# Reordering the products of a pair in the seven-product loops: B22 second, T4 after B21, the pair ends T2, T1, T3

## The chip, the core and the metric

The kernel runs on one core of a Trainium2 chip. A core has a matrix engine (TensorE, PE in the profile; its weight loads are listed apart as PEld), VectorE (DVE), ScalarE (ACT), GpSimd (POOL) and SyncE (SP, here a queue that issues transfers). Each engine works through its own list of instructions in order and waits where an operand is not ready. The metric is the device time of one execution in microseconds (us), the median of several runs; before the change it is 1209.62 us (three runs, 1209.15 to 1214.17).

## The reference

One layer of a decoder trunk is computed for 512 prompt tokens and 32 sample tokens (544 together, `NT`), width 1024, feed-forward width 2816, all in float32. The parts that the change touches are the big weight products: the input projection (keys, values, queries, convolution inputs, merge gates) and the feed-forward part.

```python
h = rmsnorm(x, w['norm1']) * (1 + sc1) + sh1
bg, cg, xin, q, kc, vc, ks, vs, kw, vw, nsa_g, merge_g = split_columns(h @ w['w_in'])
...
x = x + g1 * ((ga * y_a + gb * y_b) @ w['w_out'])
h2 = rmsnorm(x, w['norm2']) * (1 + sc2) + sh2
x = x + g2 * ((jax.nn.silu(h2 @ w['w_gate']) * (h2 @ w['w_up'])) @ w['w_down'])
```

## The kernel before

**Seven products in place of eight.** A weight slab of 256 output columns is cut into four blocks (two halves of the output columns, two halves of the contraction), the activations into four blocks (two halves of the contraction, two halves of the 544 tokens, `WH` = 272 each). Two by two blocks would take eight block products; Winograd's scheme takes seven and some sums. One slab handled so is called a pair here (it gives two times 128 output columns). The function `wpair` (L339) works one off. Its products, in three PSUM tiles: into `wA` go B11 (weights W0), then, added on top, T2 (weights WY), T3 (WZ) and T4 (W3); into `wB` goes B21 (W0); into `wC` go T1 (WY) and, on top, B22 (WZ). The names are those of the moving operands: B11, B21, B22 are blocks of the activations, T1 to T4 are sums of blocks, prepared once. W0 is two raw blocks of the slab, WY and WZ are sums of blocks that VectorE forms for each pair (tile `ws`), W3 is one raw block.

**Three matmuls for one.** To keep float32 accuracy each weight and each activation is split into a high and a low part (`to_hilo`, L393: ScalarE copies the high part, VectorE subtracts it for the low part) and `mm3` (L251) issues high x high, high x low, low x high: L252, L253, L254 in the profile. A block product is 12 matmuls of 128x272 (4 contraction chunks x 3), or 9 in the eight pairs of the down projection. A pair is 84 matmuls (63 in the down projection). In the profile `wh`/`wl` and `Wh`/`Wl` are the high and low weight tiles from two pools with two buffers each; W0 and WZ take `wh`/`wl`, WY and W3 take `Wh`/`Wl`.

**Snapshots.** `wA` is read in the middle of its accumulation: `snap` (L298) copies it with ScalarE to one of four buffers (L301 in the profile) after B11 (s1), after T2 (s2) and after T3 (s3). The next product into `wA` has to wait until the copy is done. The function `out(m, q, p, s)` finishes a quarter of the result: out(0,0) adds `wB` and s1, out(1,1) adds `wC` (holding T1 alone) and s3, out(0,1) adds `wC` (now with B22) and s2, out(1,0) takes `wA` after T4. B22 may be added to `wC` only after out(1,1) has read it. What `out` does further depends on the loop: `pair_out` (L887), `gate_out` (L1721), `up_out` (L1734), `up_seven` (L1752), `dn_out` (L1819).

**Pairs overlap.** `wpair` is a generator. Its first step issues B11 and B21, its second T2, T1 and T3; T4 and B22 are left in the generator `rest`, kept in `late[0]`, and are issued within the next pair. The callers advance `late[0]` once between the two steps (L951, L1847, L1856, L1864), which issued T4 of the last pair; `wpair` itself advances it behind T1 (L372), which issued B22 of the last pair. So the written order was B11, B21, T4 (last pair), T2, T1, B22 (last pair), T3.

**Two loops use it.** The first (L936, 23 pairs) computes the input projection in about 129 to 390 us; the second (L1840, 28 pairs) the feed-forward part in about 850 to 1156 us, with a plain product (`down_plain`) of some 45 us in it. Between them lies the attention. In the second loop six pairs of `up` form the sums of blocks of the feed-forward activations as well (`up_seven`: buffers `t0`, `t1`, `t3`, tiles `fs`, `f_x`), since the down projection is done by seven products, too.

**What sets the order.** The program is written as above, and a scheduling layer then orders the instructions of each engine by its own estimate of when operands are ready; it may bring single matmuls of a later product forward. Once built, each engine's order is fixed, and waits are semaphores. Transfers of weight slabs (`raw`, three buffers) and of prepared sums (`ws<-pre`) are issued by SP in order.

Of the kernel before, what the change touches and what calls it, by code (L numbers as in the profile page):

```python
# [14 lines left out]
ALU = mybir.AluOpType  # L15
# [23 lines left out]
WH = 272  # L39
# [117 lines left out]
def build(tc, a, o):  # L157
    nc = tc.nc
    sync, act, dve, pool, pe = nc.sync, nc.scalar, nc.vector, nc.gpsimd, nc.tensor
# [14 lines left out]
    def lin_ps(nm):  # L174
        return ps.tile([128, 512], F32, tag="g", bufs=5, name=nm)
# [12 lines left out]
    def nm(s):  # L188
        uid[0] += 1
        return f"{s}_{uid[0]}"  # L190
# [87 lines left out]
    Q = (slice(0, WH), slice(WH, NT))  # L278
# [5 lines left out]
    def seven(o_, ww, wlp, wsp):  # L284
        wi, ns, late = [0], [0], [iter(())]
        hooks = iter(o_.splits)

        def wsplit(view, odd=None):
            nk = view.shape[1]
            if odd is None:  # L290
                wi[0] += 1
                odd = wi[0] % 2
            pools = ((wpool, "wh"), (wpool, "wl")) if odd else ((ww, "Wh"), (wlp, "Wl"))
            wh, wl = (p_.tile([128, 8, 128], F32R, tag=t, bufs=2, name=nm(t))[:, 0:nk, :] for p_, t in pools)
            to_hilo(view, wh, wl)
            return wh, wl

        def snap(p):  # L298
            t = o_.snaps[ns[0] % 4]
            ns[0] += 1  # L300
            o_.snap_ops.append(act.activation(t, p, AF.Copy))  # L301
            return t

        def product(p, w, k0, X, first):
            n_ = len(X[0]) if isinstance(X[0], list) else 4
            xk = lambda t, k: t[k] if isinstance(t, list) else t[:, k, :]
            k0 *= n_
            for k in range(n_):
                mm3(p, w[0][:, k0:k0 + n_], w[1][:, k0:k0 + n_], xk(X[0], k), xk(X[1], k), k, first and k == 0, k == n_ - 1, skip_group_check=not first)

        def wslab(*key):
            n_ = len(SLABS[key][1]) // 4
            if key in pre:
                t = wsp.tile([128, 16, 128], F32, tag="ws", bufs=2, name=nm("ws"))
                sync.dma_start(t[:, n_:3 * n_].rearrange("p k f -> p (k f)"), pre[key][:, 0:256 * n_])
                y, z = t[:, 0:2 * n_], t[:, 2 * n_:4 * n_]
            else:
                y, z = (wsp.tile([128, 8, 128], F32, tag="ws", bufs=3, name=nm("ws"))[:, 0:2 * n_] for _ in range(2))
            raw = slab(*key)
            q = raw.rearrange("p k f -> p (k f)").rearrange("p (n k f) -> p n k f", n=4, k=n_)  # L320
            return q, y, z, key in pre

        def prepare(slabs):

            raw, y, z, summed = slabs
            n_ = raw.shape[2]
            y1, y2, z1, z2 = y[:, 0:n_], y[:, n_:2 * n_], z[:, 0:n_], z[:, n_:2 * n_]
            a22, a21, a11, a12 = (raw[:, i] for i in range(4))
            W0 = wsplit(raw[:, 2:4].rearrange("p n k f -> p (n k) f"))
            if not summed:  # L330
                dve.tensor_add(y2, a21, a22)
            dve.tensor_add(y1, y2, a11)
            WY = wsplit(y)
            if not summed:
                dve.tensor_add(z1, a11, a21)
            dve.tensor_add(z2, y1, a12)
            return W0, WY

        def wpair(slabs, out, ready=None, o_=o_, tie=None):  # L339

            raw, y, z, summed = slabs
            n_ = raw.shape[2]
            y1, y2, z1, z2 = y[:, 0:n_], y[:, n_:2 * n_], z[:, 0:n_], z[:, n_:2 * n_]
            a22, a21, a11, a12 = (raw[:, i] for i in range(4))
            W0 = wsplit(raw[:, 2:4].rearrange("p n k f -> p (n k) f")) if ready is None else ready[0]
            pA = s_ps(nm("wA"))[:, 0:WH]
            product(pA, W0, 0, o_.B11, True)
            s1 = snap(pA)
            pB = lin_ps(nm("wB"))[:, 0:WH]
            product(pB, W0, 1, o_.B21, True)  # L350
            out(0, 0, pB, s1)
            yield
            if ready is None:
                if not summed:
                    dve.tensor_add(y2, a21, a22)
                with tc.issue_after(tie.ins) if tie else ExitStack():
                    dve.tensor_add(y1, y2, a11)
                WY = wsplit(y)
                if not summed:
                    dve.tensor_add(z1, a11, a21)  # L360
                with tc.issue_after(tie.ins) if tie else ExitStack():
                    dve.tensor_add(z2, y1, a12)
            else:
                WY = ready[1]
            WZ = wsplit(z)
            W3 = wsplit(a22)
            product(pA, WY, 0, o_.T2, False)
            s2 = snap(pA)
            next(hooks, lambda: None)()
            pC = lin_ps(nm("wC"))[:, 0:WH]  # L370
            product(pC, WY, 1, o_.T1, True)
            next(late[0], None)  # L372
            next(hooks, lambda: None)()
            product(pA, WZ, 0, o_.T3, False)
            s3 = snap(pA)
            out(1, 1, pC, s3)
            next(hooks, lambda: None)()

            def rest():
                product(pA, W3, 0, o_.T4, False)  # L380
                out(1, 0, pA, None)
                yield
                product(pC, WZ, 1, o_.B22, False)
                out(0, 1, pC, s2)
                yield
            late[0] = rest()
            yield
        return SimpleNamespace(wsplit=wsplit, wslab=wslab, wpair=wpair, late=late, prepare=prepare)

    def hcols(hf):  # L390
        return slice(*HS[hf])

    def to_hilo(src, hi, lo):  # L393
        act.activation(hi, src, AF.Copy)  # L394
        return dve.tensor_sub(lo, src, hi.bitcast(F32))  # L395
# [304 lines left out]
    fins, late = [], []  # L700
# [29 lines left out]
    for n, (b, v) in enumerate(STEPS):  # L730
# [17 lines left out]
        if n:  # L748
            ready_ = late[:1] if n == 1 else late
            late = late[len(ready_):]  # L750
# [1001 lines left out]
    def up_seven(G, c2):  # L1752
        if c2 % 3 == 2:
            tt = [f_x[:, 4 * i:4 * i + 4] for i in range(2)]
            bb = [f_x[:, 8 + i] for i in range(6)]
        else:
            late_ = c2 % 3 == 0
            tt = [f6_tile(3 * late_ + i, [128, 4, WH], F32R, "fs") for i in range(2)]
            bb = [t[:, i] for t in (f6_tile(3 * late_ + 2, [128, 4, WH], F32R, "fs"), f6.tile([128, 2, WH], F32R, tag=f"fg{late_:d}", bufs=1, name=nm("fs"))) for i in range(t.shape[1])]
        ops = fops.setdefault((c2 - 2) // 3, {n: ([], []) for n in ("B11", "B21", "B22", "T1", "T2", "T3", "T4")})  # L1760
        for n, i in (("B11", 0), ("B21", 2), ("B22", 4)):
            for x in range(2):
                ops[n][x].append(bb[i + x])
        for n, t, i in (("T1", 0, 0), ("T3", 0, 1), ("T2", 1, 0), ("T4", 1, 1)):
            for x in range(2):
                ops[n][x].append(tt[t][:, 2 * x + i])
        Uf = flat(U)

        def out(m, q, p, s_):
            if s_ is None:  # L1770
                dve.scalar_tensor_tensor(G[:, 1, Q[0]], p, -1.0, G[:, 1, Q[0]], ALU.mult, ALU.mult)
                to_hilo(G[:, 1, Q[0]], bb[2], bb[3])
                return
            dve.tensor_add(U[:, m, Q[q]], p, s_)
            if m == 1:
                dve.scalar_tensor_tensor(G[:, 1, Q[1]], U[:, 1, Q[1]], -1.0, G[:, 1, Q[1]], ALU.mult, ALU.mult)
                to_hilo(G[:, 1, Q[1]], bb[4], bb[5])
            elif q == 1:
                dve.tensor_mul(G[:, 0, :], U[:, 0, :], G[:, 0, :])
                t0, t1, t3 = Uf[:, 0:WH], Uf[:, 2 * WH:3 * WH], Uf[:, 3 * WH:4 * WH]  # L1780
                dve.tensor_sub(t0, G[:, 0, Q[0]], G[:, 0, Q[1]])
                dve.tensor_sub(Uf[:, WH:2 * WH], G[:, 1, Q[1]], G[:, 0, Q[1]])
                to_hilo(G[:, 0, Q[0]], bb[0], bb[1])
                pair = lambda i: Uf[:, 2 * i * WH:2 * i * WH + 2 * WH].rearrange("p (k n) -> p k n", k=2)
                dve.scalar_tensor_tensor(t1, t0, -1.0, G[:, 1, Q[1]], ALU.mult, ALU.subtract)
                dve.scalar_tensor_tensor(t3, G[:, 1, Q[0]], -1.0, t1, ALU.mult, ALU.subtract)
                to_hilo(pair(0), tt[0][:, 0:2], tt[0][:, 2:4])
                to_hilo(pair(1), tt[1][:, 0:2], tt[1][:, 2:4])
        return out

    def gated(t, c, src, m, g):
# [238 lines left out]
```

## Time and profile before

| | |
|---|---|
| median of three runs | 1209.62 us |
| the profiled execution | 1209.88 us |
| its span (first to last instruction) | 1208.1 us |
| first seven-product loop | about 129 to 390 us |
| attention, output projection, first feed-forward columns | about 390 to 850 us |
| second seven-product loop | about 850 to 1156 us |
| last part of the down projection, final norm, stores | about 1156 to 1208 us |

The profile is one execution; all rows below are from it. A row of the timeline gives start, duration, engine, line, operation, output and inputs, and in brackets how long the engine was idle before it and what ended that. A row of the table by windows gives for one stretch of time its length and, for PE, PEld, DVE, ACT and POOL, the busy time and the number of instructions, then the granted clock, the share of the transfer engines and GB/s.

### The profile page before, as it was taken

What the parts mean: (1) busy time and instruction counts of PE and PEld (TensorE: products, weight loads), DVE (VectorE), ACT (ScalarE), POOL (GpSimd) and SP (SyncE); (2) the same over time, 40 slices, a digit from 0 to 9 for tenths busy, and PEclk for the clock granted to TensorE, in tenths of its full rate; (3) what the DMA queues carried; (4) which work ended last, traced back from release to release, by engine and by line L of the source; (5) the groups of instructions that cost most, each with busy time, mean ns of one, the idle gap of its engine ahead of it and who ended that gap; (6) DMA issues with size and microseconds to landing.
All of it is one profiled execution on the core that took longest, in us unless ns stands there. A gap on an engine that the chain in (4) does not pass through costs nothing. (4 is left out here: it accounts for less than half of the span.)

```text
span 1208.1 us, 25725 instructions
## 1 busy us (share of the span) xinstructions
PE 1191.2 (99%) x10114; PEld 1096.6 (91%) x10114; DVE 849.8 (70%) x1927; ACT 647.6 (54%) x1302; POOL 101.7 (8%) x154
## 2 busy tenths in 40 slices
PE   9999999999999999999999999999999999999997
PEld 7999999999999888787777879999999999999996
DVE  2539976888775576686767866758746877876776
ACT  1416544565456333386766765528555666666542
POOL 1000240000000111120101100000020001001000
PEclk9999999999999999999999999999999999999999
DMA  9953655889655998979887878534475359439512
GB/s 325 370 223 124 203 167 161 261 237 251 201 176 191 365 327 299 312 203 264 234 222 216 220 209 285 201 126 167 110 182 197 136 181 262 149 129 252 197 53 75
DMA packets 82251, 255.63 MB, mean 212 GB/s; under 512 B 9032, under 2 KB 17096, under 8 KB 67930
## 3 DMA queue, kind: packets, MB, share of 16 engines
q1 hardware_dynamic: 69442, 229.85, 54.5%
q0 software_dynamic: 12112, 23.09, 11.7%
q8 instruction: 79, 1.29, 0.4%
q10 hardware_dynamic: 576, 1.05, 0.3%
q14 instruction: 42, 0.34, 0.1%
HBM read 223.15 MB, written 65.28 MB: 239 GB/s over the span
## 5 line engine op out<-in xcount | busy, mean ns | idle before, releaser
L301 ACT ACTIVATE work<-wA 128x272 f32<-128x272 f32 x153 | 60.0, 392 | 85.3 <-PE wA L254 81.5
L395 DVE TENSOR_TENSOR Wl<-ws,Wh 128x1024 fp32r<-128x1024 f32 (+1 forms) x51 | 60.7, 1190 | 47.3 <-ACT Wh L394 44.0
L1417 ACT ACTIVATE P<-P,nms 128x384 f32<-128x384 f32 (+3 forms) x120 | 65.0, 543 | 19.8 <-DVE nms L1416 19.1
L1416 DVE CUSTOM_DVE_ANT_0 P<-sp,ta 128x384 f32<-128x384 f32 (+3 forms) x120 | 52.1, 468 | 30.0 <-PE sp L1404 22.8
L252 PE MATMUL lin<-h_h,wh 128*128 128x288 f32 (+1 forms) x240 | 71.5, 298 | 0.0
L395 DVE TENSOR_TENSOR wl<-ws,wh 128x1024 fp32r<-128x1024 f32 (+1 forms) x51 | 60.3, 1182 | 15.8 <-ACT wh L394 14.6
L253 PE MATMUL lin<-h_l,wh 128*128 128x288 f32 (+1 forms) x240 | 69.2, 289 | 0.0
L254 PE MATMUL lin<-h_h,wl 128*128 128x288 f32 (+1 forms) x240 | 68.9, 288 | 0.0
L394 ACT ACTIVATE wh<-raw 128x1024 fp32r<-128x1024 f32 (+2 forms) x55 | 55.4, 1007 | 24.1 <-PE wC L253 16.9
L394 ACT ACTIVATE Wh<-ws 128x1024 fp32r<-128x1024 f32 (+1 forms) x51 | 52.3, 1025 | 29.9 <-PE wC L253 29.2
L394 ACT ACTIVATE wh<-ws 128x1024 fp32r<-128x1024 f32 (+1 forms) x51 | 52.4, 1027 | 29.1 <-PE wB L253 27.4
L247 ACT ACTIVATE wh<-raw 128x1024 fp32r<-128x1024 f32 (+1 forms) x43 | 41.9, 973 | 43.3 <-PE lin L253 24.4
L395 DVE TENSOR_TENSOR wl<-raw,wh 128x1024 fp32r<-128x1024 f32 (+2 forms) x55 | 63.4, 1153 | 1.8 <-ACT wh L394 1.7
L658 PE MATMUL phi<-gt,wphi 128*128 128x128 f32 x512 | 61.4, 277 | 0.5 <-DMA gt<-in_cache_cmp 0.5
L658 PEld LDWEIGHTS phi<-gt,wphi 128*128 128x128 f32 x512 | 59.1, 192 | 2.7 <-DMA gt<-in_cache_cmp 1.3
L248 DVE TENSOR_TENSOR wl<-raw,wh 128x1024 fp32r<-128x1024 f32 (+1 forms) x43 | 48.2, 1121 | 16.9 <-ACT wh L247 16.4
L252 PE MATMUL wA<-S_hi,Wh 128*128 128x272 f32 x184 | 55.3, 301 | 1.7 <-ACT work L301 1.6
L557 POOL DMA_DIRECT2D pre<-in_wt x28 | 27.3, 977 | 331.0 <-DMA pre<-in_wt 331.0
L254 PE MATMUL wA<-S_hi,Wl 128*128 128x272 f32 x184 | 53.2, 289 | 0.0
L253 PE MATMUL wA<-S_lo,Wh 128*128 128x272 f32 x184 | 53.0, 288 | 0.0
L252 PEld LDWEIGHTS lin<-h_h,wh 128*128 128x128 f32 x240 | 45.6, 190 | 7.5 <-issue 6.2
L253 PEld LDWEIGHTS lin<-h_l,wh 128*128 128x128 f32 x240 | 45.2, 188 | 0.1
(583 smaller groups left out, 4365.6 us busy)
## 6 DMA issues: line engine op xcount, KB each, us to landing
raw<-in_wt SPq DMA_DIRECT2D x88, 1024.0 KB, 6.6
sraw<-in_cache_sel SPq DMA_DIRECT2D x64, 256.0 KB, 4.8
gt<-in_cache_cmp SPq DMA_DIRECT2D x60, 256.0 KB, 5.8
pre<-in_wt SPq DMA_DIRECT2D x20, 512.0 KB, 7.3
pre<-in_wt POOLq DMA_DIRECT2D x20, 512.0 KB, 7.1
ws<-pre SPq DMA_DIRECT2D x20, 512.0 KB, 3.4
raw<-in_wt SPq DMA_DIRECT2D x12, 768.0 KB, 5.7
wraw<-in_cache_winT SPq DMA_DIRECT2D x8, 1024.0 KB, 7.2
```

Of the source, the lines that this page charges most:

```text
L247: act.activation(oh, view, AF.Copy)
L248: dve.tensor_sub(ol, view, oh.bitcast(F32))
L252: pe.matmul(p, lhsT=wh[:, k, :], rhs=xh, start=start, stop=False, **kw)
L253: pe.matmul(p, lhsT=wh[:, k, :], rhs=xl, start=False, stop=False, **kw)
L254: pe.matmul(p, lhsT=wl[:, k, :], rhs=xh, start=False, stop=stop, **kw)
L301: o_.snap_ops.append(act.activation(t, p, AF.Copy))
L394: act.activation(hi, src, AF.Copy)
L395: return dve.tensor_sub(lo, src, hi.bitcast(F32))
L557: pool.dma_start(dst, src, accum_op=ALU.add)
L658: pe.matmul(po[:, c0:c0 + 128], lhsT=w[:, ch], rhs=x[:, :, ch * 16:ch * 16 + 16], start=(n_ == 0 and ch == 0), stop=(n_ == 2 and ch == 7))
L1416: p_ops.append(dve.tensor_tensor_reduce(out=t[:, 0:n], in0=sps[br], in1=t_dist[:, 512 - n:512], scale=-hs, scalar=3e38, op0=ALU.add, op1=A ...
L1417: e_ops.append(act.activation(t[:, 0:n], t[:, 0:n], AF.Exp, scale=-1.0, bias=nms[:, c:c + 1], accum_out=sums[:, c:c + 1]))
```

## The change

In the first step of `wpair`, behind B11 and its snapshot, `late[0]` is advanced once; behind T1 it is run to its end. `rest` now issues B22 first and T4 second. With the callers' advance between the steps the written order becomes B11, B22 (last pair), B21, T4 (last pair), T2, T1, T3. In `up_seven` the sums that need the result of T4 (`t3`, and the split of the second pair of sums) move from out(0,1), which came last, to out(1,0), which comes last now. No instruction is added or removed.

```diff
@@ wpair
             product(pA, W0, 0, o_.B11, True)
             s1 = snap(pA)
+            next(late[0], None)
             pB = lin_ps(nm("wB"))[:, 0:WH]
             product(pB, W0, 1, o_.B21, True)
             out(0, 0, pB, s1)
...
             product(pC, WY, 1, o_.T1, True)
-            next(late[0], None)
+            for _ in late[0]:
+                pass
             next(hooks, lambda: None)()
             product(pA, WZ, 0, o_.T3, False)
             s3 = snap(pA)
...
             def rest():
+                product(pC, WZ, 1, o_.B22, False)
+                out(0, 1, pC, s2)
+                yield
                 product(pA, W3, 0, o_.T4, False)
                 out(1, 0, pA, None)
-                yield
-                product(pC, WZ, 1, o_.B22, False)
-                out(0, 1, pC, s2)
                 yield
@@ up_seven
+        t0, t1, t3 = Uf[:, 0:WH], Uf[:, 2 * WH:3 * WH], Uf[:, 3 * WH:4 * WH]
+        pair = lambda i: Uf[:, 2 * i * WH:2 * i * WH + 2 * WH].rearrange("p (k n) -> p k n", k=2)
 
         def out(m, q, p, s_):
             if s_ is None:
                 dve.scalar_tensor_tensor(G[:, 1, Q[0]], p, -1.0, G[:, 1, Q[0]], ALU.mult, ALU.mult)
                 to_hilo(G[:, 1, Q[0]], bb[2], bb[3])
+                dve.scalar_tensor_tensor(t3, G[:, 1, Q[0]], -1.0, t1, ALU.mult, ALU.subtract)
+                to_hilo(pair(1), tt[1][:, 0:2], tt[1][:, 2:4])
                 return
...
                 dve.scalar_tensor_tensor(t1, t0, -1.0, G[:, 1, Q[1]], ALU.mult, ALU.subtract)
-                dve.scalar_tensor_tensor(t3, G[:, 1, Q[0]], -1.0, t1, ALU.mult, ALU.subtract)
                 to_hilo(pair(0), tt[0][:, 0:2], tt[0][:, 2:4])
-                to_hilo(pair(1), tt[1][:, 0:2], tt[1][:, 2:4])
```

The scheduling layer makes the following of it. The first piece is TensorE before the change, in the second loop, where `wA_1723` is the gate pair of the loop's fourth round (`c2` = 4) and `wA_1740`, `wB_1741` belong to the up pair behind it: the end of T3, then the start of the up pair.

```order
L254 MATMUL wA_1723_11850<-T3_hi_10523,wl_1728_11900 128x272
L252 MATMUL wA_1740_11984<-h2_hi_9891,wh_1738_11980 128x272
L253 MATMUL wA_1740_11984<-h2_lo_9892,wh_1738_11980 128x272
L252 MATMUL wB_1741_11998<-h2_hi_9891,wh_1738_11980 128x272
L253 MATMUL wB_1741_11998<-h2_lo_9892,wh_1738_11980 128x272
L252 MATMUL wA_1723_11850<-h2_hi_9891,Wh_1729_11903 128x272
L253 MATMUL wA_1723_11850<-h2_lo_9892,Wh_1729_11903 128x272
L254 MATMUL wA_1723_11850<-h2_hi_9891,Wl_1730_11904 128x272
L254 MATMUL wA_1740_11984<-h2_hi_9891,wl_1739_11981 128x272
```

Behind T3 stood only four matmuls of the next pair's B11 and B21 (those that need the high weights alone), and then the first three of T4 of the old pair, which go into the tile `wA_1723` whose snapshot s3 had only just been started.

The second piece is the same place after the change: the end of the up pair's B11 (its twelve matmuls stand together directly behind T3) and what follows.

```order
L252 MATMUL wA_1740_11984<-h2_hi_9891,wh_1738_11980 128x272
L253 MATMUL wA_1740_11984<-h2_lo_9892,wh_1738_11980 128x272
L254 MATMUL wA_1740_11984<-h2_hi_9891,wl_1739_11981 128x272
L252 MATMUL wC_1731_11944<-h2_hi_9891,wh_1727_11923 128x272
L253 MATMUL wC_1731_11944<-h2_lo_9892,wh_1727_11923 128x272
L254 MATMUL wC_1731_11944<-h2_hi_9891,wl_1728_11924 128x272
L252 MATMUL wC_1731_11944<-h2_hi_9891,wh_1727_11923 128x272
```

Now B22 of the gate pair (into `wC_1731`) follows B11, then the twelve of B21, and T4 stands 36 matmuls behind T3. No low-weight matmul is left out of B11 and put off.

The third piece is VectorE before the change, around the first reading of `wC_1731` by out(1,1) (L1727); `Wl` and `wl` are low-weight splits of the coming pairs.

```order
L395 TENSOR_TENSOR Wl_1743_12027<-ws_1732_11972,Wh_1742_12026 128x1024
L1774 TENSOR_TENSOR work_10832<-wC_1718_11797,work_10832 128x272
L395 TENSOR_TENSOR wl_1739_11981<-raw_1733_11974,wh_1738_11980 128x1024
L1779 TENSOR_TENSOR work_10832<-work_10832 128x544
L1727 TENSOR_TENSOR work_10832<-wC_1731_11920,work_10832 128x272
```

And after the change, the same reading, L1729 there (the file is two lines longer from here on):

```order
L1777 SCALAR_TENSOR_TENSOR work_10832<-work_10832 128x272
L397 TENSOR_TENSOR wl_1739_11981<-raw_1733_11974,wh_1738_11980 128x1024
L397 TENSOR_TENSOR fs_1705_11722<-work_10832,fs_1705_11722 128x544
L1729 TENSOR_TENSOR work_10832<-wC_1731_11944,work_10832 128x272
L397 TENSOR_TENSOR Wl_1743_12041<-ws_1732_11972,Wh_1742_12040 128x1024
```

The split `wl_1739` (W0 of the up pair) stands further ahead of the reading, with the split of the down projection's sums (`fs`) between them; the split `Wl_1743` (WY of the up pair) has gone from ahead of it to behind it. In 21 of the first loop's 23 pairs and 18 of the second loop's 28 a split of WY (`Wl<-ws`, of the coming pair) still stands directly ahead of this reading after the change.

More of the change, by code (lines that the diff above doesn't have):

```diff
@@ L1779, in out @@
                 dve.tensor_mul(G[:, 0, :], U[:, 0, :], G[:, 0, :])
-                t0, t1, t3 = Uf[:, 0:WH], Uf[:, 2 * WH:3 * WH], Uf[:, 3 * WH:4 * WH]
                 dve.tensor_sub(t0, G[:, 0, Q[0]], G[:, 0, Q[1]])
@@ L1783, in out @@
                 to_hilo(G[:, 0, Q[0]], bb[0], bb[1])
-                pair = lambda i: Uf[:, 2 * i * WH:2 * i * WH + 2 * WH].rearrange("p (k n) -> p k n", k=2)
                 dve.scalar_tensor_tensor(t1, t0, -1.0, G[:, 1, Q[1]], ALU.mult, ALU.subtract)
-                dve.scalar_tensor_tensor(t3, G[:, 1, Q[0]], -1.0, t1, ALU.mult, ALU.subtract)
                 to_hilo(pair(0), tt[0][:, 0:2], tt[0][:, 2:4])
-                to_hilo(pair(1), tt[1][:, 0:2], tt[1][:, 2:4])
         return out
```

## The prediction

> **What bounds the kernel now.** The first view is the page's busy table.
>
> ```profile
> span 1208.1 us, 25725 instructions
> ...
> PE 1191.2 (99%) x10114; PEld 1096.6 (91%) x10114; DVE 849.8 (70%) x1927; ACT 647.6 (54%) x1302; POOL 101.7 (8%) x154
> ```
>
> TensorE is the bound by far: the time can only fall where TensorE waits, and by as much as it waits there. By PE busy there is hardly anything to gain (1208.1 - 1191.2 = 16.9 us in all, the start and the end included), and the list of PE's waits, the second view, is as short:
>
> ```profile
> PE wA L252 <- ACT work L301: 2.5, 4, 1.0
> PE wA L254 <- DVE wl L395: 0.9, 2, 0.5
> PE wA L254 <- DVE Wl L395: 0.5, 2, 0.3
> ```
>
> That is 3.9 us. But a matmul's row lasts 0.29 us while the next starts 0.125 us later, so that a wait of up to 0.16 us leaves no hole in it. The third view, the table by windows, therefore matters more: it has the weight loads (second busy column), one ahead of each matmul and with less overlap.
>
> ```profile
> 153.00:390.00 237.00, 236.59 (x1878) 232.66 (x1877) 175.97 (x261) 129.05 (x195) 20.67 (x26) 1.00 0.69 204
> 930.00:1156.00 226.00, 226.00 (x1755) 221.28 (x1754) 174.47 (x299) 143.75 (x249) 13.75 (x16) 1.00 0.58 181
> 133.00:153.00 20.00, 17.89 (x135) 17.02 (x136) 19.77 (x28) 8.33 (x13) 6.93 (x7) 1.00 0.78 225
> 850.00:930.00 80.00, 78.38 (x608) 76.43 (x607) 47.46 (x77) 42.14 (x75) 6.91 (x8) 1.00 0.57 167
> 942.90:948.80 5.90, 5.90 (x49) 5.90 (x49) 4.29 (x7) 3.49 (x6) 0.00 (x0) 1.00 0.59 186
> ```
>
> The last row is a stretch inside one pair: no hole in either column. In the two steady stretches of the loops (first two rows) the loads are idle 237.00 - 232.66 = 4.34 us and 226.00 - 221.28 = 4.72 us, where PE busy shows 0.41 and 0. The timeline of one change of pairs, the fourth view, shows where.
>
> ```profile
> 948.74 0.29 PE L254 MATMUL wA<-T_hi,wl 128*128 128x272 f32 x1
> 948.87 0.29 PE L252 MATMUL wA<-h_hi,wh 128*128 128x272 f32 x1
> 949.00 0.29 PE L253 MATMUL wA<-h_lo,wh 128*128 128x272 f32 x1
> 949.07 0.40 ACT L301 ACTIVATE work<-wA 128x272 f32<-128x272 f32 x1 [0.57 <-PE wA L254]
> 949.12 0.29 PE L252 MATMUL wB<-h_hi,wh 128*128 128x272 f32 x1
> 949.25 0.28 PE L253 MATMUL wB<-h_lo,wh 128*128 128x272 f32 x1
> 949.52 0.19 PEld L252 LDWEIGHTS wA<-h_hi,Wh 128*128 128x128 f32 x1 [0.21 <-ACT work L301]
> 949.52 0.39 PE L252 MATMUL wA<-h_hi,Wh 128*128 128x272 f32 x1
> 949.75 0.29 PE L253 MATMUL wA<-h_lo,Wh 128*128 128x272 f32 x1
> 949.88 0.29 PE L254 MATMUL wA<-h_hi,Wl 128*128 128x272 f32 x1
> ```
>
> T3 ends with the first row. Its snapshot s3 can start only at 949.07 and ends at 949.47; T4's first matmul, four places behind T3, waits for it until 949.52. It starts 0.27 us after the one ahead instead of 0.125, and the next comes 0.23 us later instead of 0.125: 0.145 + 0.105 = **0.25 us lost per change of pairs**, of which the load's row shows 0.21.
>
> A rule of the Trainium skill bears on each of these two points. Its page "Perfetto Trace Analysis", section "Identifying the Most-Contended Engine", says that matmul busy time is no measure of TensorE's headroom and that the busy share of LDWEIGHTS should be used. By matmul busy the change could win 3.9 us at most, by the loads some 10; the rows above bear the rule out. Its page "TensorE: Matmul & The Clock Gate", section "Step-by-step: what each phase is for", says that TensorE pulls a weight load ahead of running matmuls when it goes to the background buffer. By that rule the second of the two losses would not be there, the first term of the sum below would be 10.8 x 0.145/0.25 = 6.3 us and the time 1206.8; here the load at 949.52 waited along with its matmul and the next start took 0.23 us, so the measurement decides against it.
>
> **The change, part by part.** Nothing is added or removed; each part is a wait that goes or comes.
>
> *T4 behind B21* (both loops). T4 moves from 4 to 6 matmuls behind T3 to 36, or 4.5 us, and the snapshot needs 949.52 - 948.87 = 0.65 us from T3's end. This wait goes in every pair. So do the waits for W0's low part (`PE wA L254 <- DVE wl`) that come with it: B22 of the pair before, whose weights held the buffer of the coming W0, comes 48 matmuls or 6 us earlier. Scaled by 0.25/0.21 the idle times are 4.34 x 1.19 = 5.2 and 4.72 x 1.19 = 5.6: **-10.8 us** in the steady stretches.
>
> *B22 in second place* brings a new wait. B22 is added to `wC`, which out(1,1) must have read, and that reading needs s3. Let T be the start of the first matmul behind T3. B22 is due at T + 12 x 0.125 = T + 1.51. s3 ends at T + 0.60 (949.47 against 948.87), and a reading right behind it would take 0.43 us and be over at T + 1.06. But in 39 of 51 pairs a split of WY stands directly ahead of the reading on VectorE, and it waits for T1. What that costs, the timeline has:
>
> ```profile
> 945.74 0.29 PE L254 MATMUL wC<-T_hi,Wl 128*128 128x272 f32 x1
> 945.94 1.06 ACT L394 ACTIVATE Wh<-ws 128x1024 fp32r<-128x1024 f32 x1 [0.67 <-PE wC L253]
> 947.03 1.23 DVE L395 TENSOR_TENSOR Wl<-ws,Wh 128x1024 fp32r<-128x1024 f32 x1 [1.56 <-ACT Wh L394]
> 948.18 0.43 DVE L1774 TENSOR_TENSOR work<-wC,work 128x272 f32<-128x272 f32 x1
> ```
>
> The first row is T1's last matmul; the next product starts at 945.87. From there the copy starts 0.07 later, the split 1.09 after that, the reading 1.15 after that, takes 0.43, and TensorE can go on 0.05 later (as 949.52 follows 949.47): 2.79 us. T3 takes 1.51 of them after the change, so B22 can start at T + 1.28, due at T + 1.51. **0.23 us of slack**: enough, unless ScalarE or VectorE holds one more operation in between. In the eight pairs of the down projection B11, T1 and T3 are 9 matmuls; T3 and B11 cover 2.26 us instead of 3.02, the split is 128x768 in six of them: between 0 and 0.5 us late, and 0.1 for the restart. I take 0.25 each, 2.0. Of the other 43 I take ten as late by 0.1, with 0.1 for the restart: 2.0. Together **+4.0 us**; the bounds are 0 and 51 x 0.25 = 12.8.
>
> *T3 directly behind T1.* T3 needs s2, and B22 no longer stands between. T1 is 12 matmuls, 1.51 us, the snapshot 0.65: 0.86 us of slack, less than one copy of 1.06 us on ScalarE. I count nothing (bounds 0 and 0.3 in a quarter of the pairs, 4).
>
> *The start of the first loop.* The row 133 to 153 has VectorE busy for 19.77 of 20 us. TensorE's long wait there:
>
> ```profile
> 150.37 0.43 DVE L891 TENSOR_TENSOR work<-wC,work 128x272 f32<-128x272 f32 x1
> 150.89 0.40 ACT L301 ACTIVATE work<-wA 128x272 f32<-128x272 f32 x1 [1.62 <-DVE work L891]
> 151.34 0.39 PE L252 MATMUL wA<-S_hi,Wh 128*128 128x272 f32 x1 [1.03 <-ACT work L301]
> ```
>
> s3 was held up by a reading of `wC` on VectorE: snapshots rotate through four buffers, three are taken per pair, so s3 overwrites the s2 of the pair before, which out(0,1) reads behind B22. With B22 early this link is gone, but the new reading ahead of B22 queues behind the same splits on a full VectorE. I count 0 (bounds -1.6 and +1).
>
> *The restart after the plain product* (850 to 930, 80 - 76.43 = 3.57 us idle). There TensorE waits for weights that came late and, from 924 on, for the copies and splits behind them:
>
> ```profile
> 924.00:930.00 6.00, 5.43 (x37) 4.55 (x36) 5.22 (x10) 3.72 (x8) 0.00 (x0) 1.00 0.70 236
> ...
> 924.63 0.39 PE L252 MATMUL wA<-T_hi,wh 128*128 128x272 f32 x1
> 926.53 0.39 PE L252 MATMUL wA<-h_hi,wh 128*128 128x272 f32 x1
> 927.68 0.39 PE L252 MATMUL wA<-h_hi,Wh 128*128 128x272 f32 x1 [0.39 <-ACT work L301]
> ```
>
> The first wait for weights stays; 6.00 - 4.55 = 1.45 of the 3.57 us lie behind 924, and with B22 done during the first wait part of this goes; I take half: **-0.8** (bounds -1.5, +1).
>
> *SP and GpSimd.* Moved results send their stores and loads at other times; a slab is loaded three pairs ahead, so I count nothing. The same for the sums moved in `up_seven`: the same operations on VectorE, which has 25% to spare in these stretches (174.47 of 226.00), and their readers come pairs later. The attention and the tail keep their work: 0 (bounds -1.5, +1.5).
>
> Sum: -10.8 + 4.0 - 0.8 = **-7.6 us**. From the profiled execution, 1209.88 us (the median of the runs is 1209.62, so nothing to correct): **1202.3 us**.
>
> **The rivals.**
> 1. *The wait only changes its name.* B22's slack of 0.23 us is used up in nearly every pair: one operation of 0.43 us on VectorE between split and reading makes it 0.2 late, with the restart 0.3, as much as was saved. For it: VectorE's order is made from estimates, and it is 70% busy. Against it: the split is mostly directly ahead of the reading in the order. In 40 pairs 0.25 each: 1209.9 - 10.8 + 10 = about 1209. Chance 0.18.
> 2. *PE busy is right* and the loads' holes are no lost time: at most the 3.9 us, 1206. Against it: the starts 0.27 and 0.23 apart. Chance 0.07.
> 3. *More goes.* No new waits, the start of the loop and the restart gain too: 1209.9 - 10.8 - 1.6 - 0.8 = 1196.7. Chance 0.12.
> 4. *Slower:* a split of 1.15 us slips in front of the reading just as s3 ends, so that the reading starts at T + 0.60 + 1.15 and B22 at T + 2.23, 0.72 late and 0.1 for the restart. It decides from a reading later than T + 1.03. In 30 of the 51 pairs: 30 x 0.82 = 24.6, less 10.8: 1224. Against it: the split there waits for T1, not s3, and so starts 0.9 us before. Chance 0.05.
>
> **How the numbers follow.** My forecast, 1199 to 1205, has 0.58. About 0.5% (1203.6 and 1215.7) is what a measurement of this kernel can tell from no change. Of my case some four fifths lies under 1203.6, with rival 3 this makes faster 0.58; slower is rival 4, 0.05; the rest, 0.37, is within. The range for 8 in 10 reaches from near rival 3 to rival 1, whose upper half, most of rival 3 and rival 4 are left out: 1197.5 to 1209.
>
> **What would show it.** The loads' idle time in the two steady stretches falls from 4.3 and 4.7 us to under 2 each; no T4 matmul starts over 0.15 us after the one ahead; pairs of 84 matmuls follow at 10.55 us. Wrong would be: first matmuls of B22 that start 0.2 us late behind a reading of `wC` in most pairs (rival 1), or T3's behind s2; or holes that go without the span getting shorter (rival 2).

## The result, and the profile after

The change made the kernel slower: 1223.15 us in the median of seven runs (1219.32 to 1229.26) against 1212.01 us for the kernel before, run beside it (1209.15 to 1214.17), a ratio of 1.0098 with a 95% interval of 1.0072 to 1.0124. The profiled execution took 1224.94 us. The first lines of its page:

```profile
span 1223.2 us, 25697 instructions
...
PE 1192.9 (98%) x10114; PEld 1102.0 (90%) x10114; DVE 851.8 (70%) x1927; ACT 646.4 (53%) x1302; POOL 103.9 (8%) x154
```

All engines are busy for nearly as long as before; the span is 15.1 us longer. So TensorE waits more, or runs slower for a while. Both are the case. The list of PE's waits after the change (in total, times, longest):

```profile
PE wC L252 <- DVE work L1780: 6.1, 2, 3.9
PE wC L252 <- DVE work L1825: 3.9, 4, 1.9
PE wC L252 <- DVE work L895: 3.2, 4, 2.1
PE wC L252 <- DVE work L1747: 2.9, 1, 2.9
...
PE wA L252 <- ACT work L301: 1.1, 2, 0.6
```

The wait for the snapshots (last row) has shrunk from 2.5 us, as foreseen. The four rows on `wC` are new: B22's first matmul waits until VectorE has read `wC` in out(1,1), eleven times and 16.1 us in all. The table by windows (length; busy time of PE, PEld, DVE, ACT, POOL with counts; granted clock; share of the transfer engines; GB/s) says in which loop:

```profile
153.00:390.00 237.00, 235.40 (x1889) 233.68 (x1890) 175.53 (x264) 127.83 (x194) 20.31 (x24) 1.00 0.65 204
850.00:930.00 80.00, 75.11 (x575) 73.81 (x575) 45.42 (x76) 41.33 (x72) 6.92 (x8) 0.98 0.53 155
930.00:1156.00 226.00, 216.90 (x1667) 213.93 (x1666) 170.03 (x286) 136.38 (x237) 13.76 (x16) 0.98 0.57 178
```

The weight loads' idle time fell in the first loop, from 4.34 to 237.00 - 233.68 = 3.32 us, and rose in the second, from 4.72 to 12.07 and around the plain product from 3.57 to 6.19. The granted clock, 1.00 in all these rows before, is 0.98 in the two last.

I number the pairs from 0; 0 to 22 are the first loop, 23 to 50 the second. From the first matmul of B11 of one pair to that of another, before and after: pairs 0 to 22 took 249.4 and 248.4 us, 22 to 23 (with the attention) 471.5 and 472.4, 23 to 50 294.1 and 309.9. The loss lies in the second loop. The quiet pairs (those without a long wait) are faster than before: the last seven of the first loop take 10.56 us each instead of 10.83, and in the second loop every other one 10.55 instead of 10.79. A few are far slower: 17.14 us from pair 27 to 28, 14.55 from 37 to 38, 16.41 from 47 to 48.

### The profile page after: what moved, and what is told of

The parts are those of the page before. It is cut to its first block, busy times and chain, and to the rows that moved or that the text cites. A ratio compares the mean times of both kernels' runs of the same rounds, so it can differ in the third digit from the quotient of the medians.

```text
span 1223.2 us, 25697 instructions
## 1 busy us (share of the span) xinstructions
PE 1192.9 (98%) x10114; PEld 1102.0 (90%) x10114; DVE 851.8 (70%) x1927; ACT 646.4 (53%) x1302; POOL 103.9 (8%) x154
## 5 line engine op out<-in xcount | busy, mean ns | idle before, releaser
L358 DVE TENSOR_TENSOR ws<-ws,raw 128x512 f32<-128x512 f32 (+1 forms) x50 | 34.2, 684 | 32.7 <-DMA ws<-pre 26.9
```

## One long wait, row by row

The timeline of VectorE, SP and TensorE around the second of these, where pair 36's B22 starts (columns as before):

```profile
1012.90 1.23 DVE L397 TENSOR_TENSOR wl<-ws,wh 128x1024 fp32r<-128x1024 f32 x1 [0.58 <-ACT wh L396]
1014.15 0.32 SPq L315 DMA_DIRECT2D ws<-pre  x1
1019.65 0.69 DVE L358 TENSOR_TENSOR ws<-ws,raw 128x512 f32<-128x512 f32 x1 [3.34 <-DMA ws<-pre]
1020.38 0.69 DVE L363 TENSOR_TENSOR ws<-ws,raw 128x512 f32<-128x512 f32 x1
1020.98 1.22 DVE L397 TENSOR_TENSOR Wl<-ws,Wh 128x1024 fp32r<-128x1024 f32 x1
1022.12 0.43 DVE L1780 TENSOR_TENSOR work<-wC,work 128x272 f32<-128x272 f32 x1
1022.61 0.39 PE L252 MATMUL wC<-h_hi,wh 128*128 128x272 f32 x1 [2.21 <-DVE work L1780]
```

Read it upward. B22 (last row) waited for the reading of `wC`. The reading was not late by its own operand; it stood in VectorE's queue behind a split of WY and two additions (L358, L363), and the first addition sat idle for 3.34 us for the transfer `ws<-pre`, issued 5.50 us earlier, at once after the low split of WZ (first row) had given its buffer free. VectorE's order names the pairs: the additions go into `ws_1840`, the tile of pair 38, the split belongs to pair 37 (`ws_1827`), the reading to pair 36 (`wC_1826`).

```order
L358 TENSOR_TENSOR ws_1840_12886<-ws_1840_12886,raw_1841_12888 128x512
L363 TENSOR_TENSOR ws_1840_12886<-ws_1840_12886,raw_1841_12888 128x512
L397 TENSOR_TENSOR Wl_1834_12833<-ws_1827_12755,Wh_1833_12832 128x1024
L1780 TENSOR_TENSOR work_10832<-wC_1826_12725,work_10832 128x272
```

So a sum for a pair whose first matmul is still 13.6 us away (1033.27) holds up a reading that TensorE is waiting for. Before the change the same queue could do no harm, since B22 came 48 matmuls, 6 us, behind the place where it now stands.

The wait is not the whole price. Two rows of the table by windows, one ahead of that wait and one behind it:

```profile
1018.00:1020.00 2.00, 2.00 (x18) 2.00 (x18) 0.35 (x1) 0.78 (x2) 0.00 (x0) 1.00 1.06 361
1023.40:1026.40 3.00, 3.00 (x15) 3.00 (x15) 1.59 (x4) 1.15 (x2) 0.00 (x0) 0.50 0.26 108
```

The granted clock is 0.50 in the second (half speed), and matmuls start 0.227 us apart instead of 0.126. It happens behind the waits at 920.8, 1022.6 and 1126.6, for 13, 14 and 24 matmuls: 51 x 0.101 = 5.2 us.

Added up over the 4116 matmuls of the products, the time from one start to the next was 534.8 us before and is 549.2 us now. The difference, 14.3 us, is nearly all of the 15.1 us by which the span is longer.

## The experiments

Theory A: the reading of `wC` stands on VectorE behind additions that wait for their transfer, and the long waits then bring half-speed matmuls. The rivals: the transfer is too late for whatever comes next (B), VectorE has too much to do (C), T4's new place costs the time (D). A second question came with the runs: whether what the steady pairs gained was really T4's place.

| run | median, us | ratio to before, 95% interval |
|---|---|---|
| the change | 1223.15 | 1.0098 (1.0072 to 1.0124) |
| e1, products in written order, hold on additions | 1217.37 | 1.0048 (1.0032 to 1.0063) |
| e2, B22 third | 1206.57 | 0.9952 (0.9933 to 0.9971) |
| e3, products in written order only | 1234.51 | 1.0186 (1.0168 to 1.0205) |
| e4, before, products in written order | 1244.76 | 1.0268 (1.0246 to 1.0291) |
| e5, before, B22 ahead of T1 | 1202.92 | 0.9931 (0.9919 to 0.9943) |
| e6, hold in three pairs | 1221.07 | 1.0083 (1.0059 to 1.0106) |
| e7, B22 third, hold in one pair | 1206.26 | 0.9950 (0.9936 to 0.9965) |
| e8, no accumulating transfers | 1208.92 | 0.9977 (0.9966 to 0.9988) |
| e9, hold behind the pair before last | 1211.38 | 0.9983 (0.9969 to 0.9998) |
| e10, e2 with the hold of e9 | 1201.39 | 0.9912 (0.9898 to 0.9926) |
| e11, waits made longer | 1248.61 | 1.0300 (1.0279 to 1.0320) |

### e3 and e1: the written order alone, and the hold

Both fix the order of TensorE's products; `tc.issue_after(x)` puts what is inside it behind x in the schedule.

```diff
-            for k in range(n_):
-                mm3(...)
+            with tc.issue_after(last[0].ins) if last[0] else ExitStack():
+                for k in range(n_):
+                    r = mm3(...)
+            last[0] = r
```

> The changed kernel with the products held in the order of the text and nothing else: the control for the run that also holds WY behind the reading. In the changed kernel 1 to 8 matmuls of B21 stand ahead of B22 in some pairs around the down pairs; here none do. Theory A: no gain, rather 0 to 5 us more since B22 starts up to 1 us earlier there, 1221 to 1230 us. Rival E (the split products, with their extra weight loads and broken groups, are the cost): 1205 to 1215.

e1 adds, with `read[-1]` set to the reading of `wC` by the outputs of the first loop, of `up` and of the down projection:

```diff
-                with tc.issue_after(tie.ins) if tie else ExitStack():
+                with tc.issue_after(tie.ins) if tie else ExitStack(), tc.issue_after(read[-1].ins) if read[-1] else ExitStack():
                     dve.tensor_add(y1, y2, a11)
```

> The changed kernel with two edits: the products of the seven-product pairs are held in the order of the text (each behind the one before), and the first addition that prepares the next pair's WY is held behind VectorE's reading of wC in out(1,1). Theory A (the reading stands on VectorE behind the next pair's WY, which waits for its transfer ws<-pre; the long waits then bring half-speed matmuls): B22's waits of 4.19, 2.50, 3.22 and 2.19 us and their slow stretches go, T2 has 36 matmuls (4.5 us) after B22's start and hides the transfer, so 1200 to 1208 us, ratio to before 0.990 to 0.997, clock 0.998. Rival B (the transfer itself comes too late for whatever needs it): the wait moves from B22 to T2, 1218 to 1225. Rival C (VectorE has simply too much to do behind T3): no change, 1220 to 1228.

e3 took 1234.51 us, the sign that theory A gave and 4.5 us more than it allowed. In the changed kernel the scheduler has put up to 6 matmuls of B21 ahead of B22 around the down pairs, which cover part of the wait; in written order B22 waits longer. Rival E of the expectation, that these split products are the cost, falls. PE's waits of e3:

```profile
PE wC L252 <- DVE work L1828: 10.7, 7, 3.6
PE wC L252 <- DVE work L1783: 5.5, 3, 3.4
PE wC L252 <- DVE work L1732: 5.4, 4, 2.2
```

and of e1, which differs from it by the hold alone:

```profile
PE wA L254 <- DVE wl L403: 11.0, 12, 2.6
PE wA L252 <- ACT work L305: 3.3, 2, 2.8
...
PE wC L252 <- DVE work L1735: 1.1, 1, 1.1
```

22.2 us of B22's waits (with 0.6 from the first loop) became 1.1, and the time fell by 17.1 us. The wait is thus for what stands ahead of the reading; VectorE has the same to do in both runs, so C falls as its explanation. But e1 stayed well above the 1200 to 1208 expected. 11.0 us now go to low splits that stand in the queue behind the additions that were moved back: eight of the twelve waits, 6.9 us, are for W0's, four, 4.0 us, for WZ's. So a part of the wait moved, as rival B had it, though not to T2. The 2.8 us of the second row lie at the start of the first loop, where e3 has the same wait, and come with the written order. `gate_out` sets no `read`, so that the hold was the last pair's reading for a gate pair and that of the pair before last for an `up` pair. The former was later than needed.

### e6 and e7: a hold that was put on the wrong pair

```diff
-        gate = wpair(wslab("fg", c2), gate_out(G), tie=last_mod[0] if c2 == 1 else None)
+        gate = wpair(wslab("fg", c2), gate_out(G), tie=last_mod[0] if c2 == 1 else read[0] if c2 in (3, 6, 9) else None)
```

`read[0]` is the last reading of `wC` by `up`.

> The changed kernel with one edit: in three pairs (the gates of c2 = 3, 6 and 9) the additions that prepare WY and WZ are held behind VectorE's reading of the last pair's wC; no product is held. Theory A: the waits of 4.19, 2.50 and 3.22 us go (9.5 us beyond the normal pitch), and with them the 51 matmuls at 0.227 us (5.1 us), the waits in the down pairs stay: 1206 to 1211 us. Rival (the slow stretches come from something else than the waits): 1211 to 1215. Rival B (the transfer is waited for by whatever comes next): 1219 to 1225.

> The run with B22 third, and in one pair (the gate of c2 = 3) the additions for WY and WZ held behind VectorE's reading of the last pair's wC. Theory A: the one wait of 2.48 us that was left at B22 goes, 1203 to 1205 us. Rival B (the transfer is waited for by T2 instead): 1206 to 1207.

Neither came out: 1221.07 us, and 1206.26 us where the same order without the hold had 1206.57. VectorE's timeline in e6, at the place shown above, tells why:

```profile
1019.21 0.69 DVE L360 TENSOR_TENSOR ws<-ws,raw 128x512 f32<-128x512 f32 x1 [3.88 <-DMA ws<-pre]
1019.93 0.69 DVE L365 TENSOR_TENSOR ws<-ws,raw 128x512 f32<-128x512 f32 x1
1020.54 0.43 DVE L1783 TENSOR_TENSOR work<-wC,work 128x272 f32<-128x272 f32 x1
1020.89 0.68 DVE L360 TENSOR_TENSOR ws<-ws,raw 128x512 f32<-128x512 f32 x1
```

There are two additions of L360 now. The held one (1020.89, pair 37) did go behind the reading. The one that waits for the transfer is pair 38's and still stands ahead of it. I had taken the additions for those of the next pair; they are of the pair after the next. In e7 the wait went to W0's low split (2.6 us, the longest in its list). Both times lie where rival B had put them, but with the hold on the wrong pair the runs can't tell A from B; that is left to e9 and e10.

### e9: the hold on the right pair

`read` now gets every reading of `wC`, the gate's too, and the additions are held behind the one of the pair before last:

```diff
+                hold = tie or read[-2]
...
-                with tc.issue_after(tie.ins) if tie else ExitStack():
+                with tc.issue_after(hold.ins) if hold else ExitStack():
                     dve.tensor_add(y1, y2, a11)
...
-                with tc.issue_after(tie.ins) if tie else ExitStack():
+                with tc.issue_after(hold.ins) if hold else ExitStack():
                     dve.tensor_add(z2, y1, a12)
```

> The changed kernel with one edit: in every pair VectorE's additions for WY and WZ are held behind its reading of wC for the pair before last (the trace of the last run with a hold shows that the additions that wait for ws<-pre belong to the pair after the next, so the two earlier holds, on the next pair's additions, were put on the wrong pair). No product is held; the order of the products is that of the changed kernel but for 12 matmuls of B21 in the down pairs. Theory A: no reading waits for a transfer, B22's waits of 4.19, 2.50, 3.22 and 2.19 us fall below 0.7 us each, the 51 slow matmuls go, clock 0.998, spread of the runs under 6 us instead of 10: 1202 to 1209 us. Rival C (VectorE has too much to do behind T3 anyway): waits of 1 us and more stay at those places, 1214 to 1222.

1211.38 us: 11.8 us less than the changed kernel, but 2.4 us above the expected range, and the runs spread over 9 us, not under 6. In the second loop no wait of B22 on a reading is left over 0.8 us, where rival C had waits of 1 us and more staying. The one of 2.1 us in the first loop stayed; there VectorE is at work without a pause from 145 to 153 us, and theory C holds for that place. The rest of what is missing goes to others that stand behind the waiting addition. From e9's list of waits:

```profile
PE wA L252 <- ACT work L303: 4.0, 4, 1.5
PE wA L254 <- DVE wl L400: 2.2, 2, 1.2
PE wC L252 <- DVE work L898: 2.1, 1, 2.1
```

and from its timeline, ahead of the snapshot with one of the two long waits in the first row (1.4 us, at 1002.82; the other is 1.5):

```profile
998.06 0.69 DVE L361 TENSOR_TENSOR ws<-ws,raw 128x512 f32<-128x512 f32 x1 [2.65 <-DMA ws<-pre]
...
999.87 0.52 ACT L1803 ACTIVATE dsp<-dsp,modT 128x272 f32<-128x272 f32 x1 [2.19 <-DVE dsp L1831]
1000.30 1.04 ACT L399 ACTIVATE wh<-raw 128x1024 fp32r<-128x1024 f32 x1
...
1002.39 0.38 ACT L303 ACTIVATE work<-wA 128x272 f32<-128x272 f32 x1
```

VectorE waits for the transfer, ScalarE for VectorE, and the snapshot stands in ScalarE's queue behind both. Theory A holds for B22's waits, and rival B for a part of what is left; the hold chooses who stands behind the late transfer, it does not make it earlier.

### e2 and e10: B22 one product later

```diff
             s1 = snap(pA)
-            next(late[0], None)
             pB = lin_ps(nm("wB"))[:, 0:WH]
             product(pB, W0, 1, o_.B21, True)
             out(0, 0, pB, s1)
+            next(late[0], None)
             yield
```

> The changed kernel with one edit: the last pair's B22 stands behind B21 instead of ahead of it (B11, B21, last B22, last T4, T2, T1, T3). Theory A: B22 starts 12 matmuls (1.5 us) later, and B21, WZ and with it the issue of the next ws<-pre come 1.5 us earlier; the long waits of 4.19, 2.50, 3.22, 2.19 us shrink by 1.5 to 3 us each and those near 1 us go, so 1203 to 1212 us, with at most two waits over 1 us at B22. Rival C (VectorE has too much to do in every pair): the waits shrink by 1.5 us once each but stay in place, 1214 to 1220. Rival D (the new last place of T4, not B22, costs the time, since up_seven's sums now wait for T4): no change, 1220 to 1227.

1206.57 us: as theory A had it, and below the kernel before. T4 and the sums of `up_seven` stand as late as in the changed kernel, so D falls. One wait of 2.2 us at B22 was left, at 919.6 us. e10 puts the hold of e9 on it.

> The run with B22 third, with the same hold. Theory A: the last long wait at B22 (2.48 us) goes: 1202 to 1205 us, equal to the run with B22 ahead of T1 within 2 us. Rival (that wait comes from the accumulating transfers that read U, behind which W0's split stands in this pair): 1206 to 1208, the wait moves to W0.

1201.39 us, the lowest time of all, 0.6 us below the range and within 2 us of e5, as expected. TensorE's longest waits at B22 and at W0 are 0.4 and 0.8 us in its list, so with one product more of cover hardly anything waits for the transfer, and B falls as the main cause. In e10's windows the loads are idle for 2.00, 2.34 and 0.54 us, and the clock is 1.00:

```profile
153.00:390.00 237.00, 236.39 (x1898) 235.00 (x1899) 177.55 (x265) 129.69 (x198) 22.93 (x28) 1.00 0.68 210
850.00:930.00 80.00, 78.86 (x618) 77.66 (x618) 50.25 (x84) 44.97 (x78) 6.92 (x8) 1.00 0.57 167
930.00:1156.00 226.00, 226.00 (x1793) 225.46 (x1792) 177.23 (x304) 144.37 (x251) 13.97 (x16) 1.00 0.59 184
```

### e4 and e5: what the steady pairs had been waiting for

e4 is the kernel before with its products held in written order, as in e3: T4 stands whole behind B21.

> The kernel before, its order kept (B11, B21, last T4, T2, T1, last B22, T3), with one edit: every product is held behind the one before it, so that T4 starts whole behind B21, 24 matmuls after T3, and not 4 matmuls after it. It measures the term of T4's wait alone (10.8 us in the prediction). If that term is right and nothing is late behind it: 1199 to 1205 us, ratio 0.988 to 0.994, and the steady pairs fall from 10.8 to 10.55 us. Rival: the matmuls of T4 and T1 drawn ahead filled a wait for W0's low split, which now stands at B11 or B21 instead: 1207 to 1214.

1244.76 us: the rival was right, and by more than it said. The top of e4's list of waits, and its timeline at one change of pairs in the first loop:

```profile
PE wA L254 <- DVE wl L398: 26.0, 43, 1.3
```

```profile
309.60 0.29 PE L254 MATMUL wC<-h_h,wl 128*128 128x272 f32 x1
309.80 1.06 ACT L397 ACTIVATE wh<-raw 128x1024 fp32r<-128x1024 f32 x1 [0.45 <-PE wC L253]
310.89 1.23 DVE L398 TENSOR_TENSOR wl<-raw,wh 128x1024 fp32r<-128x1024 f32 x1
...
312.17 0.19 PEld L254 LDWEIGHTS wA<-h_h,wl 128*128 128x128 f32 x1 [0.75 <-DVE wl L398]
```

The first row is the end of B22 of the pair before last. Its weights lie in the tile that the coming W0 gets. Only then does ScalarE cast W0 (1.06 us) and VectorE split it (1.23), done at 312.12; the T3 between covers 1.5 us of it, and B11's first matmul with low weights waits. Quiet pairs take 11.37 us. So in the kernel before the early matmuls of T4 and T1 were what the scheduler had put into this hole: T4 lost 0.25 us there, and without it a quiet pair takes 11.37 us instead of 10.83. (Holding all products, as e4 does, cost the changed kernel 11 us in e3, so the 32 us lost here need not all be this wait; the list has 26.0 of it.) e5 takes the cause away: it moves B22 from behind T1 to ahead of it and leaves T4 first.

```diff
             product(pA, WY, 0, o_.T2, False)
             s2 = snap(pA)
+            next(late[0], None)
             next(hooks, lambda: None)()
             pC = lin_ps(nm("wC"))[:, 0:WH]
             product(pC, WY, 1, o_.T1, True)
-            next(late[0], None)
             next(hooks, lambda: None)()
```

> The kernel before with one edit: the last pair's B22 stands one product earlier, ahead of T1 instead of behind it (B11, B21, last T4, T2, last B22, T1, T3). T4 keeps its place, first of the two. Theory W (what the steady pairs lost was not T4's place but the wait for W0: W0's tile is the one that B22 of the pair before last read, B22 ended 1.5 us ahead of B11, and cast and low split need 2.4 us): B22 now ends 3.0 us ahead of B11, the wait goes, T4 starts whole behind B21, pairs at 10.55 us, and no reading is near: 1198 to 1204 us, ratio 0.988 to 0.994, which is also below the run with B22 third. Rival (T4's place is the term, as the prediction had it): T4 stays within 4 matmuls of T3 or waits again, pairs at 10.8, 1208 to 1213 us.

1202.92 us, inside the range of theory W. T4 stands whole behind B21, quiet pairs take 10.57 us in the first loop and 10.55 in the second, and W0's cast and split, in e5's timeline,

```profile
306.73 1.06 ACT L394 ACTIVATE wh<-raw 128x1024 fp32r<-128x1024 f32 x1 [0.98 <-PE wC L253]
307.82 1.22 DVE L395 TENSOR_TENSOR wl<-raw,wh 128x1024 fp32r<-128x1024 f32 x1 [0.53 <-ACT wh L394]
```

are done at 309.04, 0.9 us before the first matmul with them (309.93).

### e8: why the transfer was late

```diff
     def add_x1(m, t):
-        pool.dma_start(x1_dr[m], t, accum_op=ALU.add)
+        pass
```

> The changed kernel without GpSimd's accumulating transfers of the down products into the residual (the down products are computed but not added, so the end of the computation lacks them; all else is as in the changed kernel). It asks why the transfer ws<-pre takes 8 us at the long waits against a median of 3.3. Theory T1 (the accumulating transfers share the DMA engines with it): the transfer takes 3 to 5 us there, the waits at B22 around and in the down pairs shrink to under 1 us each, 1206 to 1211 us. Theory T2 (it is issued too late, since WZ's split waits for B21, which now stands 1.5 us later): the waits stay within 0.5 us each, 1219 to 1226 us.

1208.92 us, inside the range of T1; B22's waits in the down pairs and right behind them are 0.8 us or less, and one of 1.4 us is left at pair 47. (This kernel leaves out part of the result, so it is no candidate.) At the place of the long wait the same steps take

```profile
1006.58 0.32 SPq L315 DMA_DIRECT2D ws<-pre  x1
...
1010.09 0.69 DVE L358 TENSOR_TENSOR ws<-ws,raw 128x512 f32<-128x512 f32 x1 [1.35 <-DMA ws<-pre]
```

3.51 us from issue to addition in place of 5.50; at the other two long waits 3.60 in place of 8.63 and 3.40 in place of 6.23. In the changed kernel the transfers' table of the stretch from 1014 to 1020 us (packets, MB, share of the 16 engines) has

```profile
q1 hardware_dynamic: 218, 1.11, 51.1%
q0 software_dynamic: 181, 0.34, 41.2%
```

The accumulating transfers of the down projection, alone in the second queue, move under a quarter of the bytes and take two fifths of the engines' time. That is why the long waits lie beside the plain product and the down pairs. The run doesn't separate all of it: without these transfers VectorE is also spared a wait on `U`, which they read around 910 us. That the 16 engines serve all queues alike is what the Trainium skill says (page "DMA: Bandwidth & Descriptors", section "Issuing engines are not separate DMA queues"); these rows agree.

### e11: the price of a wait

```diff
-    def pair_out(G, done):
+    def pair_out(G, done, times=1):
...
-                dve.scalar_tensor_tensor(g_, p, -1.0, s_, ALU.mult, ALU.subtract)
+                for _ in range(times):
+                    dve.scalar_tensor_tensor(g_, p, -1.0, s_, ALU.mult, ALU.subtract)
...
-pair_out(G7[n % 3], done)
+pair_out(G7[n % 3], done, {12: 4, 14: 5, 16: 6, 18: 8, 20: 12}.get(n, 1))
```

> The changed kernel with longer waits made on purpose, to price a wait: in the first loop, where the granted clock was 1.00, VectorE's reading of wC in out(1,1) is repeated (4, 5, 6, 8 and 12 times in pairs 12, 14, 16, 18 and 20, with the same result), and B22, which overwrites wC, waits for all of them; the products of that loop are held in the order of the text. At 0.36 us for a repeat the waits come to about 2.3, 2.7, 3.0, 3.7 and 5.2 us. Theory H (a long wait is what brings the matmuls at 0.227 us): those of 2.8 us and more are followed by 12 to 25 matmuls at 0.227 us (1.2 to 2.5 us more each), that of 2.3 us perhaps not, so 17 us of waits and 5 to 9 us of slow matmuls, 1240 to 1255 us. Rival (the slow matmuls have to do with the second loop's own load): pitches of 0.126 us behind all five, 1235 to 1243 us.

1248.61 us. The waits came to 2.89, 2.76, 3.24, 4.19 and 6.09 us from start to start, and half speed followed each, for 14, 13, 14, 22 and 12 matmuls. Rows of e11's windows, a stretch without a wait and three behind one:

```profile
272.00:284.00 12.00, 11.47 (x89) 11.03 (x88) 10.70 (x20) 6.73 (x11) 0.00 (x0) 1.00 0.82 273
...
312.10:314.90 2.80, 2.80 (x14) 2.80 (x14) 0.10 (x1) 0.33 (x1) 0.88 (x1) 0.50 0.43 37
339.30:342.30 3.00, 3.00 (x15) 3.00 (x15) 1.74 (x3) 1.34 (x2) 0.00 (x0) 0.50 0.94 207
364.90:369.60 4.70, 4.70 (x23) 4.70 (x22) 1.65 (x2) 1.06 (x1) 0.00 (x0) 0.50 0.76 144
```

The first came out longer than meant (2.3), so none is short enough to show from which length on it happens. The pair with the wait of 2.76 us took 14.84 us instead of 10.56, 4.28 more, of which the wait is 2.63 and the 13 slow matmuls 13 x 0.101 = 1.3. That half speed has to do with the second loop's own load is excluded, since it came here in the first loop, behind waits that were put there; theory H stands.

## Why the prediction was wrong

**The step that failed** is "*B22 in second place*", +4.0 us, with its conclusion "**0.23 us of slack**: enough, unless ScalarE or VectorE holds one more operation in between". VectorE held more: the additions of the pair after the next, and they wait for a transfer. The working followed the reading back to T1 through one row ahead of it in VectorE's order and stopped there. In the trace before no reading of `wC` was waited for, so that no wait pointed at the transfer. But the order that the text counted from had it: in the changed kernel an addition for the pair after the coming one stands directly ahead of that split in 15 of the 18 pairs of the second loop. "*SP and GpSimd* ... I count nothing" is the same omission a second time: the transfer that mattered is not the slab, loaded three pairs ahead, but `ws<-pre`, whose tile has two buffers and which is issued only when WZ of two pairs earlier is split. At the three long waits it took 5.5 to 8.6 us from issue to the addition.

In place of +4.0 the runs show for the second loop: seven waits at B22 of 0.66 to 4.19 us, together 15.0 us (14.1 above the usual pitch), and 5.2 us of matmuls at half speed behind three of them. In the first loop four waits of 0.51 to 2.41 us add 3.9 us above the pitch; there VectorE's own work is the cause of the longest. That makes 23.2 us, of which 14.3 are left in the sum over all products, so the rest of the change gained about 9 us.

**"T4 behind B21", -10.8 us**: the size was about right, the order of the causes wrong. Quiet pairs fell to the 10.55 us that the text named, though in the second loop only every other one. Where nothing new stands in the way the term is seen in the total: e5 gained 1211.87 - 1202.92 = 9.0 us. But T4's distance from T3 was not the cause by itself: e4 put T4 whole behind B21 and became slower. The text named W0's wait as something that goes "with it"; it was the first cause, and T4's early place the scheduler's cure for it. The gain comes from an earlier B22. The sixth place became the fifth in e5 and the third in e2, and both gained; the change chose the second, where B11 and T3 alone stand between T1 and B22.

**"T3 directly behind T1", 0**: right, the snapshots' waits fell to 1.1 us. **The start of the first loop, 0 (up to +1)**: pairs 0 to 4 took 48.8 us against 47.8, so +1.1, at the bound. **The restart after the plain product, -0.8**: wrong, the longest wait of all (4.19 us) lies there, by the failed step.

**The rivals.** The fourth named VectorE's queue, the sign and by luck the time (1224), but as 30 small delays of 0.82 us from one extra split. There were few and large ones, and the queue was long because its head waited. With 0.05 its chance was too low: the text itself had 0.23 us of slack on a queue whose contents it had read for one row. The half-speed clock was in no case.

## What to carry to other kernels

An instruction is as late as the latest operand of everything ahead of it on its engine. When a consumer is moved closer to its producer, read the engine's order behind the producer for the rows that belong to other, later work, and ask of each what transfer it needs and how long that takes beside the traffic of that stage, not at the median. And when a scheduler has put odd single matmuls early, look for the hole that they fill before counting their waits as loss: here the hole was a weight tile's release, and moving the product that releases it by one place gave 9 us, while taking the filler away exposed 26 us of waits.

## What the runs showed of the hardware

The clock's reaction to short waits was new to me. In the profiles of the two kernels and the eleven runs there are 17 waits of TensorE of 2.76 us or more (from start to start, ahead of a matmul of these products); all 17 are followed, within 0.5 to 1.9 us, by 12 to 25 matmuls at 0.227 us, half speed. Of 14 waits between 2.0 and 2.5 us (two of them in the plain product) six are. Of 16 waits between 1.4 and 1.95 us that stand alone (all matmuls from 60 to 1190 us) none is, but two of 1.46 and 0.72 us that lie within 2 us of each other in e9 are. In e3 two waits of 2.17 us differ in this: one is followed by half speed, the other isn't. The Trainium skill (page "TensorE: Matmul & The Clock Gate", section "What's actually happening") puts the halving behind an idle window of about 3.4 us which runs freely; that it runs freely agrees with the two equal waits, while the waits of 2.1 to 2.9 us that were enough here are shorter than the window named, and by these runs 2 us is the length to stay under.

The price goes by stretches. In the clock's record every stretch at 0.50, but for the one at the kernel's end, lasts 3.41 or 6.83 us: in the changed kernel 3.41 us from 920.85 and from 1023.25 and 6.83 us from 1125.65. So a wait of 2.5 us cost as many slow matmuls (14) as one of 4.19 us (13).

The spread of the runs fits, too: the changed kernel's seven runs differ by 10 us at mean clocks of 0.990 to 0.996, while e10's four differ by 1.5 us at 0.997 to 0.998.
